# A two-layer hybrid trunk on one core: row vectors spread through DRAM, embedding blocks behind each gate, norm weights applied at PSUM

## The chip, the cores and the metric

The kernel runs on one core of one Trainium2 chip. The metric is the device time of one execution in microseconds (us). A core has a matrix engine (TensorE, PE in the profile; its weight loads are PEld), a vector engine (VectorE, DVE), an activation engine (ScalarE, ACT), a general engine (GpSimd, POOL) and queues that issue DMAs; here the queues of SyncE (SP) and of POOL are used. SBUF is the on-chip memory of 128 partitions, PSUM the memory that TensorE writes.

## The reference

256 tokens go through two layers of width 2048, batch 1. Each layer normalises, projects, mixes along the sequence, multiplies by a gate, projects back and adds; behind it comes a gated per-layer embedding.

```python
for i in range(DEPTH):                       # DEPTH = 2
    hn = rmsnorm(h, e_norm[j] if i % 2 == 0 else o_norm[j])
    if i % 2 == 0:                           # HGRN2 heads and RG-LRU blocks side by side
        qa, fa, ia, za, xb, zb = split(hn @ e_w_in[j])
        ya = head_rmsnorm(hgrn2(qa, fa, ia, lbs[j]), a_norm[j]) * silu(za)
        yb = rg_lru(causal_conv(xb, ...), ...) * silu(zb)
        mix = concat(ya, yb) @ e_w_out[j]
    else:                                    # mLSTM with a running-max stabiliser
        qk, v, og, z, ig, fg = split(hn @ o_w_in[j])
        q, k = split(silu(causal_conv(qk, ...)))
        yc = mlstm(q, k, v, ig + c_b_i[j], log_sigmoid(fg + c_b_f[j]))
        yc = head_rmsnorm(yc, c_norm[j]) * sigmoid(og) * silu(z)
        mix = yc @ o_w_out[j]
    h = h + mix
    pl = rmsnorm(p[i] @ ple_w[i], ple_norm[i])        # p[i]: 256 tokens x 256
    h = h + sigmoid(h @ ple_gate_w[i]) * pl
return rmsnorm(h, final_norm)
```

All of it is float32.

## The kernel before

Every weight comes from DRAM in raw halves of 128x1024 float32 through the SP queue (`raw`). ACT rounds a half to a shorter type (`whi`, L122) and DVE takes the rest (`wlo`, L123); activations are split likewise (`ahl`). A product is then three matmuls: hi×hi, hi×lo, lo×hi.

There are two shapes of product. `block` makes 128 features of all 256 tokens: 16 matmuls of 512 columns with `whi` (L153, both parts of the activation at once), a `pump()`, and 16 of 256 columns with `wlo` (L159). `project_tok` makes 512 features token by token, in two halves of 128 tokens; its matmuls of 512 columns are L194, L195 and L196.

Work beside the products is written as Python generators, called lanes: `start(name, gen)` enters one, `pump()` advances every lane by one `yield`, `drain(name)` runs one to its end. `pump()` is called once in each block and each group of `project_tok`, so a `yield` puts the next step about one block later. A tile scheduler and the order of the code set the order on each engine; an engine takes its instructions in that order, and waits at the head of its queue.

PSUM has three pools of 2 KB banks: `mm` (three banks, for the products), `mx` (three, for small products and transposes) and `st` (two).

What the change touches, in the order of time:

- Row norms. A norm factor is made with one token per partition (`rcr`). `to_free` lays it along the free axis on all partitions: DVE multiplies a diagonal (`dg`, L231), PE multiplies it by ones (L234), and `free_copy` copies the bank to SBUF on ACT (L262). It is used three times: `hrs` in layer 0 (first read by L176), `plrs` for the embedding of layer 0 (read by POOL, L341), `hrs` in layer 1 (first read at L835).
- Attention of layer 0. `attention(g)` makes the matrix `A` of two head groups; part of it, the cross-half product (L617 to L620), goes to a third `mx` bank. `read_out` multiplies the output `o` by its row norms `r` on POOL (L660). Beside it DVE runs the four-tap convolution (`xc`, L718), the products of the RG-LRU with its scan (`tt`, L706), and the weight subtractions; ACT waits for the scan in L688; PE's next product of `xc` is L684.
- The mixer of layer 1. Gate statistics give the running max `Mx` of eight heads (DVE, L844). `split8` rounds it into two parts (L242, L243), and for each head pair j `mix(j)` spreads two of its rows over all partitions with four matmuls by a column of an identity (`spread`, L250 and L251, into an `mx` bank); DVE then takes `wt` from it (L872).
- The `oz` gates of layer 1. For j = 0 to 3 `gate_tok` makes a gate `u` (DVE, L455), DVE multiplies it by the mixer's output (L981), and the lane `fm` (`feature_major`) transposes it on PE (L438, into `mx`) and evacuates it on ACT (L446) and DVE (L447) into `ahl`, which out_proj's blocks read. `embed(g)` makes 512 features of the embedding of layer 1, twelve matmuls in two halves (L964 to L966, into `mm`); DVE copies each half to `pl` (L968), ACT sums its squares (L970). Behind the gates POOL loads the embedding's norm row with `row` (L949, 512 KB each) and multiplies the eight halves by it (L993); the sums of squares are added on DVE (`total`, L999) and inverted.

The order around the gates, before:

```python
            start("fm", feature_major(u, "cn", 4 * j, y))
            if j in (1, 2):
                embed(j - 1)
        embed(2)
        pump()
        embed(3)
        drain("fm")
        pnr = row(0)
        ...
        act = out_proj(hq, a["oo"], y)
```

Of the kernel before, what the change touches and what calls it, by code (L numbers as in the profile page):

```python
# [19 lines left out]
P = 128  # L20
T = 256
# [23 lines left out]
def trunk(ctx: ExitStack, tc: tile.TileContext, a, out):  # L45
# [17 lines left out]
    def start(lane, gen):  # L63
        lanes.setdefault(lane, []).append(gen)
# [80 lines left out]

    def block(w, act):


        ps = pm.tile([P, 512], F32, name="mm", tag="mm")
        parts = load_weights(w)  # L150
        for k in range(KT):
            c = (k % 8) * P
            last["pe"] = te.matmul(ps, parts[k // 8][0][:, c:c + P],  # L153
                                   act[k // 2][2][:, (k % 2) * 512:(k % 2 + 1) * 512],
                                   start=(k == 0), stop=False).ins
        pump()
        for k in range(KT):
            c = (k % 8) * P
            last["pe"] = te.matmul(ps[:, T:2 * T], parts[k // 8][1][:, c:c + P], act[k // 2][0][:, k % 2],  # L159
                                   start=False, stop=(k == KT - 1)).ins  # L160
        return ps
# [65 lines left out]

    def to_free(rt):

        dg = tp.tile([P, T], F32, name="dg", tag="dg", bufs=1)  # L230
        v.tensor_tensor(out=dg.rearrange("p (h t) -> p h t", h=2), in0=ident.unsqueeze(1).to_broadcast([P, 2, P]),  # L231
                        in1=rt.unsqueeze(2).to_broadcast([P, 2, P]), op=ALU.mult)
        st = pst.tile([P, 512], F32, name="st", tag="st")
        te.matmul(st[:, 0:T], ones[:, 0:P], dg, start=True, stop=True)  # L234
        return st[:, 0:T]

    def split8(x, name):

        n = x.shape[0]
        hi = tp.tile([8, T], F32R, name=name + "h", tag="s8h", bufs=1)[0:n, :]  # L240
        lo = tp.tile([8, T], F32R, name=name + "l", tag="s8l", bufs=1)[0:n, :]
        v.tensor_copy(hi, x)  # L242
        v.tensor_tensor(out=lo, in0=x, in1=hi.bitcast(F32), op=ALU.subtract)  # L243
        return hi, lo

    def spread(o, parts, h):

        n = parts[0].shape[0]
        w = identr[0:n, h:h + 1].to_broadcast([n, P])
        te.matmul(o, w, parts[0], start=True, stop=False)  # L250
        te.matmul(o, w, parts[1], start=False, stop=True)  # L251

    def folded(acc, *more):
# [5 lines left out]
    def free_copy(rt, name):  # L259
        ps = to_free(rt)  # L260
        rs = tp.tile([P, T], F32, name=name, tag="rsb")
        s.copy(rs, ps)  # L262
        return rs
# [80 lines left out]

    def out_proj(hq, w, y):

        act = []
        for j in range(8):
            for i in range(2):
                ps = block(w[2 * j + i], y)  # L350
# [44 lines left out]
    pls = ple(load_p(0), p0, lambda: sy.dma_start(out=prm, in_=a["prm"]))  # L395
    identr = cp.tile([8, 8], F32R, name="identr")
    acc = cp.tile([P, 512], F32, name="acc", tag="acc")
# [62 lines left out]
    def derive():  # L460
        sy.dma_start(out=cst, in_=a["cst"])
        v.tensor_copy(identr, ident[0:8, 0:8])
        yield
# [33 lines left out]
    with m0_scope:  # L497
# [35 lines left out]
        A = m0.tile([P, 8, P], F32, name="A", tag="A", bufs=1)  # L533
        gp.memset(A, 0.0)

        def attention(g):
# [70 lines left out]
            for b in range(2):  # L607
# [8 lines left out]
                banks.append(p3)  # L616
            ps = px.tile([P, 512], F32, name="mx", tag="mx")  # L617
            for c in range(4):
# [19 lines left out]
        def read_out(g, A, Ac, vt):  # L638
# [20 lines left out]
            o8 = o.rearrange("p h (c e) -> p (h c) e", c=4)  # L659
            gp.tensor_tensor(out=o8, in0=o8, in1=r.unsqueeze(2).to_broadcast([P, 8, P]), op=ALU.mult)  # L660
            res["o", g] = o
# [107 lines left out]
    with tc.tile_pool(name="m1", bufs=2) as m1:  # L769
# [59 lines left out]
        def gate_stats(ps):  # L829
# [16 lines left out]
            s.activation(enm, enm, AF.Exp, scale=-1.0)  # L846
            pM.append(split8(Mx, "Mx"))
            yield
# [14 lines left out]
        den, ss, fac = (m1.tile([P, 16], F32, name=n, bufs=1) for n in ("den", "ss", "fac"))  # L863

        def mix(j):

            ps = px.tile([P, 512], F32, name="mx", tag="mx")
            for i in range(2):
                spread(ps[:, i * T:(i + 1) * T], pM[0], 2 * j + i)
            p3 = ps.rearrange("p (i t) -> p i t", i=2)  # L870
            wt = m1.tile([P, 2, 384], F32, name="wt", tag="wt", bufs=1)
# [3 lines left out]
            for i in range(2):  # L875
                hd = 2 * j + i
                s.activation(wt[:, i, 0:T], wt[:, i, 0:T], AF.Exp, bias=aT[:, hd:hd + 1])
                s.activation(wt[:, i, T:384], wt[:, i, T:384], AF.Exp, bias=aT[:, 8 + hd:9 + hd])
            yield
            yield  # L880
# [74 lines left out]

        def embed(g):
            hi, lo = load_weights(a["pw1"][g // 2], halves=(g % 2,))[0]
            halves = []
            for hf in range(2):
                ps = pm.tile([P, 512], F32, name="mm", tag="mm")  # L960
                for k in range(2):
# [5 lines left out]
                pl = m1.tile([P, 512], F32, name="pl", tag="qk", bufs=8)  # L967
                v.tensor_copy(pl, ps)  # L968
                sq = tp.tile([P, 512], F32, name="sq", tag="sq")
# [4 lines left out]
        for j in range(4):  # L974
# [8 lines left out]
            start("fm", feature_major(u, "cn", 4 * j, y))  # L983
            if j in (1, 2):
                embed(j - 1)
        embed(2)
        pump()
        embed(3)
        drain("fm")
        pnr = row(0)  # L990
        for g in range(4):
            for pl in pls[g]:
                gp.tensor_tensor(out=pl, in0=pl, in1=pnr[g // 2][:, (g % 2) * 512:(g % 2 + 1) * 512], op=ALU.mult)  # L993
        fnr = row(1)

# [7 lines left out]
        rp = m1.tile([P, 2], F32, name="rp", bufs=1)  # L1003
        v.tensor_scalar(rp, rsqrt_cols(total(pss, 4)), 0.5, None, op0=ALU.mult)

        act = out_proj(hq, a["oo"], y)


# [195 lines left out]
```

## Time and profile before

| what | value |
|---|---|
| median of 3 runs (lowest to highest) | 1090.41 us (1090.06 to 1091.36) |
| the profiled execution | 1090.81 us, its span 1089.0 us |
| mean granted TensorE clock | 0.997 |
| PE busy | 1064.6 us, 98% of the span |
| DVE, ACT, POOL busy | 753.4, 580.8, 86.5 us (69%, 53%, 8%) |
| mean traffic | 184 GB/s; the 16 DMA engines are 40% to 80% busy by slice |

A line of the timeline has the start in us from the span's start, the time of the group in us, engine, line, operation, the tile written and the tiles read, shapes, and how many instructions the group has; in brackets stands how long the engine was idle before it, and what ended that. Consecutive matmuls overlap in their records, so what one costs is the distance from its start to the next one's. A line of groups has the count, then busy time and the mean duration in ns, then the idle time before. Where three durations stand with slashes, they are the shortest, the median and the longest.

### The profile page before, as it was taken

To read this page: it belongs to the slowest core of one execution; us is meant where nothing else is said; L and a number is where in the kernel's file an instruction comes from. 1 tells how busy PE (TensorE), PEld (TensorE's weight loads), DVE (VectorE), ACT (ScalarE), POOL (GpSimd) and SP (SyncE) were. 2 spreads that over 40 slices of the span, in tenths; PEclk is the share of its full clock that TensorE was granted. 3 is DMA by queue.
4 is the path that set the end of the run, shared out by engine and by line. 5 is a ranking of instruction groups with operands and counts; after the bars stand their busy time and mean duration, and the time that the engine had idled before them with its cause. 6 is when DMAs were issued, how large, how long until landed. Compare 5 with 4: busy or idle time off the path is not lost.

```text
span 1089.0 us, 16844 instructions
## 1 busy us (share of the span) xinstructions
PE 1064.6 (98%) x6522; PEld 913.0 (84%) x6522; DVE 753.4 (69%) x1121; ACT 580.8 (53%) x850; POOL 86.5 (8%) x74
## 2 busy tenths in 40 slices
PE   7999999999999999999999999999999999999996
PEld 6788888887888888888888888888888878888886
DVE  7968978877767556877544877764456686655565
ACT  6565455688654435555444656644445554434543
POOL 2142200000000000112000000000000120000111
PEclk9999999999999999999999999999999999999998
DMA  8655544446755555555554544445555665555552
GB/s 322 204 193 193 176 161 140 148 136 194 236 198 186 192 192 192 187 186 184 190 193 166 180 156 157 163 168 194 196 190 199 217 202 177 183 189 175 192 174 78
DMA packets 55952, 200.31 MB, mean 184 GB/s; under 512 B 6208, under 2 KB 6592, under 8 KB 55872
## 3 DMA queue, kind: packets, MB, share of 16 engines
q1 hardware_dynamic: 54720, 195.04, 53.0%
q0 software_dynamic: 1152, 4.19, 1.2%
q8 instruction: 51, 0.84, 0.3%
q14 instruction: 29, 0.24, 0.1%
HBM read 197.11 MB, written 2.10 MB: 183 GB/s over the span
## 4 chain that ended last, share of the span: by engine, by line
PE 89%; DVE 5%; ACT 4%; issue 1%; DMA 1%; SPq 0%; DVEq 0%; ACTq 0%
PE mm L153 31%; PE mm L159 17%; PE mm L194 12%; PE mm L196 12%; PE mm L195 12%; DVE wlo L123 2%; ACT whi L122 1%; PE mm L1058 1%; PE mm L1056 1%; PE mm L1057 1%; DMA raw<-in_pw_dram 1%; PE nu L897 1%; PE mx L556 1%; DVE ahl L138 0%; ACT L695 0%
## 5 line engine op out<-in xcount | busy, mean ns | idle before, releaser
L123 DVE TENSOR_TENSOR wlo<-raw,whi 128x1024 fp32r<-128x1024 f32 (+1 forms) x361 | 450.7, 1273 | 244.8 <-ACT whi L122 136.1
L122 ACT CAST whi<-raw 128x1024 fp32r<-128x1024 f32 (+1 forms) x361 | 377.1, 1047 | 331.8 <-PE mm L153 171.8
L153 PE MATMUL mm<-ahl,whi 128*128 128x512 f32 x1536 | 367.7, 392 | 2.7 <-DVE ahl L447 1.9
L153 PEld LDWEIGHTS mm<-ahl,whi 128*128 128x128 f32 x1536 | 282.3, 188 | 59.1 <-DVE ahl L447 3.0
L194 PE MATMUL mm<-whi,ahl 128*128 128x512 f32 x608 | 239.8, 394 | 2.4 <-DVE u L455 1.9
L196 PE MATMUL mm<-whi,ahl 128*128 128x512 f32 x608 | 237.1, 390 | 1.8 <-DVE ahl L138 1.8
L195 PE MATMUL mm<-wlo,ahl 128*128 128x512 f32 x608 | 237.2, 390 | 0.8 <-DVE wlo L123 0.8
L159 PE MATMUL mm<-ahl,wlo 128*128 128x256 f32 x1536 | 202.4, 285 | 0.0
L159 PEld LDWEIGHTS mm<-ahl,wlo 128*128 128x128 f32 x1536 | 195.4, 191 | 6.2
L194 PEld LDWEIGHTS mm<-whi,ahl 128*128 128x128 f32 x608 | 114.3, 188 | 27.6 <-DVE u L455 3.1
L196 PEld LDWEIGHTS mm<-whi,ahl 128*128 128x128 f32 x608 | 114.2, 188 | 27.0 <-DVE ahl L138 3.1
L195 PEld LDWEIGHTS mm<-wlo,ahl 128*128 128x128 f32 x608 | 114.3, 188 | 23.9 <-DVE wlo L123 1.1
L165 ACT COPY sm<-mm 128x256 f32<-128x256 f32 x64 | 23.7, 371 | 45.0 <-PE mm L159 45.0
L271 POOL TENSOR_TENSOR acc<-acc,sq 128x512 f32<-128x512 f32 x11 | 19.9, 1812 | 212.6 <-ACT sq L270 212.4
L166 DVE TENSOR_TENSOR mg<-mm,sm 128x256 f32<-128x256 f32 x64 | 26.7, 418 | 0.0
L782 DVE SCALAR_TENSOR_TENSOR qk<-mg,prm,qk 128x255 f32<-128x255 f32 (+2 forms) x48 | 21.3, 479 | 6.8 <-ACT qk L779 6.5
L949 POOL DMA_DIRECT2D row<-in_rows_dram x4 | 2.2, 553 | 279.8 <-DVE u L981 268.1
L1044 POOL TENSOR_TENSOR pl<-pl,row 128x512 f32<-128x512 f32 x6 | 9.2, 1533 | 153.7 <-ACT sq L1028 153.7
L446 ACT ACTIVATE ahl<-mx,prm 128x256 fp32r<-128x256 f32 x24 | 10.9, 473 | 14.6 <-PE mx L438 8.3
L1056 PE MATMUL mm<-whi,ahl 128*128 128x256 f32 x64 | 18.3, 286 | 0.0
L138 DVE TENSOR_TENSOR ahl<-hq,ahl 128x512 fp32r<-128x512 f32 x16 | 10.7, 690 | 10.8 <-ACT ahl L137 10.8
L1057 PE MATMUL mm<-wlo,ahl 128*128 128x256 f32 x64 | 18.1, 283 | 0.0
(299 smaller groups left out, 822.8 us busy)
## 6 DMA issues: line engine op xcount, KB each, us to landing
raw<-in_ew_dram SPq DMA_DIRECT2D x64, 512.0 KB, 4.8
raw<-in_g_dram SPq DMA_DIRECT2D x56, 512.0 KB, 4.3
raw<-in_eo_dram SPq DMA_DIRECT2D x32, 512.0 KB, 4.6
raw<-in_ov_dram SPq DMA_DIRECT2D x32, 512.0 KB, 4.1
raw<-in_oqk_dram SPq DMA_DIRECT2D x32, 512.0 KB, 4.5
raw<-in_oog_dram SPq DMA_DIRECT2D x32, 512.0 KB, 4.2
raw<-in_oz_dram SPq DMA_DIRECT2D x32, 512.0 KB, 4.1
raw<-in_oo_dram SPq DMA_DIRECT2D x32, 512.0 KB, 4.6
```

Of the source, the lines that this page charges most:

```text
L122: last["act"] = s.copy(h, r).ins
L123: last["dve"] = v.tensor_tensor(out=l, in0=r, in1=h.bitcast(F32), op=ALU.subtract).ins
L153: last["pe"] = te.matmul(ps, parts[k // 8][0][:, c:c + P], act[k // 2][2][:, (k % 2) * 512:(k % 2 + 1) * 512], start=(k == 0), stop=False).ins
L159: last["pe"] = te.matmul(ps[:, T:2 * T], parts[k // 8][1][:, c:c + P], act[k // 2][0][:, k % 2], start=False, stop=(k == KT - 1)).ins
L165: s.copy(small, ps[:, T:2 * T])
L166: v.tensor_tensor(out=dst, in0=ps[:, 0:T], in1=small, op=ALU.add)
L194: te.matmul(ps[hf], xh, wh, start=(k == 0), stop=False)
L195: te.matmul(ps[hf], xh, wl, start=False, stop=False)
L196: last["pe"] = te.matmul(ps[hf], xl, wh, start=False, stop=(k == KT - 1)).ins
L782: v.scalar_tensor_tensor(dst[:, sh:T], pi[:, 0:T - sh], pc("ccw", k * 16 + b), dst[:, sh:T], op0=ALU.mult, op1=ALU.add)
L1056: te.matmul(ps[hf], xh, wh, start=(k == 0), stop=False)
L1057: te.matmul(ps[hf], xh, wl, start=False, stop=False)
```

## The change

`to_free`, `split8`, `spread` by matmul and the identity for it are gone. `free_copy` and the mixer's spread write the row vector to a DRAM tile and read it back with every partition reading the same bytes, both on POOL's DMA queue. `mix(0)` has one more `yield` ahead of its work, and the spread of pair j + 2 is asked for when pair j's `wt` is done. `embed(j)` stands behind each gate j and writes `st` banks; its norm row is loaded per block (256 KB, `pnr`) and multiplied where the bank is evacuated, so POOL's eight products are gone. The row of the final norm, the sums and the inversion go into a lane that runs during out_proj. The last gate's `fm` lane is finished within out_proj's first block, which runs twelve hi matmuls, then the lane, then the rest. The cross-half product of attention writes an `st` bank, and the product of `o` with its row norms is made by DVE. Line numbers after the change differ by up to 15: L153 is L155, L159 is L162, L123 is L124, L438 is L427, L447 is L436, L455 is L444, L718 is L707, L706 is L695, L964 to L966 are L969 and the next.

```diff
-    def block(w, act):
+    def block(w, act, mid=None):
...
+        if mid is None:
+            his(range(KT))
+            pump()
+            los(range(KT))
+        else:
+            his(range(12))
+            mid()
+            los(range(12))
+            his(range(12, KT))
+            los(range(12, KT))
         return ps
...
     def free_copy(rt, name):
-        ps = to_free(rt)
+        d = dr.tile([T], F32, name=name + "d", tag="rsd")
+        gp.dma_start(out=d.rearrange("(h p) -> p h", h=2), in_=rt)
         rs = tp.tile([P, T], F32, name=name, tag="rsb")
-        s.copy(rs, ps)
+        gp.dma_start(out=rs, in_=d.partition_broadcast(P))
         return rs
...
-            ps = px.tile([P, 512], F32, name="mx", tag="mx")
+            ps = pst.tile([P, 512], F32, name="st", tag="st")
             for c in range(4):
                 cc = slice(c * P, (c + 1) * P)
                 te.matmul(ps[:, cc], kx[:, cc], qx[:, cc], start=True, stop=True)
...
-            gp.tensor_tensor(out=o8, in0=o8, in1=r.unsqueeze(2).to_broadcast([P, 8, P]), op=ALU.mult)
+            v.tensor_tensor(out=o8, in0=o8, in1=r.unsqueeze(2).to_broadcast([P, 8, P]), op=ALU.mult)
...
-            pM.append(split8(Mx, "Mx"))
+            d = dr.tile([8, T], F32, name="Mxd", tag="Mxd")
+            gp.dma_start(out=d, in_=Mx)
+            pM.append(d)
...
+        def spread(j):
+            t = m1.tile([P, 2, T], F32, name="spr", tag="spr", bufs=2)
+            gp.dma_start(out=t, in_=pM[0][2 * j:2 * j + 2].partition_broadcast(P))
+            spr[j] = t
+
         def mix(j):
 
-            ps = px.tile([P, 512], F32, name="mx", tag="mx")
-            for i in range(2):
-                spread(ps[:, i * T:(i + 1) * T], pM[0], 2 * j + i)
-            p3 = ps.rearrange("p (i t) -> p i t", i=2)
+            if j == 0:
+                spread(0)
+                spread(1)
+                yield
+            p3 = spr[j]
...
+            if j < 2:
+                spread(j + 2)
...
         def embed(g):
+            pnr = m1.tile([P, 512], F32, name="pnr", tag="spr", bufs=2)
+            gp.dma_start(out=pnr, in_=a["rows"][0, g * 512:(g + 1) * 512].partition_broadcast(P))
...
-                ps = pm.tile([P, 512], F32, name="mm", tag="mm")
+                ps = pst.tile([P, 512], F32, name="st", tag="st")
...
-                v.tensor_copy(pl, ps)
+                v.tensor_tensor(out=pl, in0=ps, in1=pnr, op=ALU.mult)
...
-            if j in (1, 2):
-                embed(j - 1)
-        embed(2)
+            embed(j)
         pump()
-        embed(3)
-        drain("fm")
-        pnr = row(0)
-        for g in range(4):
-            for pl in pls[g]:
-                gp.tensor_tensor(out=pl, in0=pl, in1=pnr[g // 2][:, (g % 2) * 512:(g % 2 + 1) * 512], op=ALU.mult)
-        fnr = row(1)
+        pump()
+        pump()
+        rows = []
...
-        v.tensor_scalar(rp, rsqrt_cols(total(pss, 4)), 0.5, None, op0=ALU.mult)
-
-        act = out_proj(hq, a["oo"], y)
+        def embed_norm():
+            yield
+            yield
+            rows.extend(row(1))
+            v.tensor_scalar(rp, rsqrt_cols(total(pss, 4)), 0.5, None, op0=ALU.mult)
+            yield
+
+        start("en", embed_norm())
+        act = out_proj(hq, a["oo"], y, lambda: drain("fm"))
+        drain("en")
+        fnr = rows
```

On PE, at the end of the gates of layer 1, the order before the change is this: the last embedding block, the transposes of `u` between and behind its matmuls, and out_proj's first two blocks.

```order
L438 MATMUL mx<-cst,u 128x128
L964 MATMUL mm<-whi,ahl 128x512
L965 MATMUL mm<-wlo,ahl 128x512
L966 MATMUL mm<-whi,ahl 128x512
L964 MATMUL mm<-whi,ahl 128x512
L965 MATMUL mm<-wlo,ahl 128x512
L966 MATMUL mm<-whi,ahl 128x512
L438 MATMUL mx<-cst,u 128x128 x5
L153 MATMUL mm<-ahl,whi 128x512 x21
L159 MATMUL mm<-ahl,wlo 128x256 x16
L153 MATMUL mm<-ahl,whi 128x512 x11
L159 MATMUL mm<-ahl,wlo 128x256 x16
```

At the same place on PE after the change:

```order
L427 MATMUL mx<-cst,u 128x128 x2
L155 MATMUL mm<-ahl,whi 128x512 x6
L427 MATMUL mx<-cst,u 128x128 x3
L155 MATMUL mm<-ahl,whi 128x512 x5
L427 MATMUL mx<-cst,u 128x128 x3
L155 MATMUL mm<-ahl,whi 128x512
L162 MATMUL mm<-ahl,wlo 128x256 x12
L155 MATMUL mm<-ahl,whi 128x512 x9
L162 MATMUL mm<-ahl,wlo 128x256 x4
L155 MATMUL mm<-ahl,whi 128x512 x11
L162 MATMUL mm<-ahl,wlo 128x256 x16
```

The transposes now stand among out_proj's first twelve hi matmuls, in pieces of two, three and three, and the four remaining hi matmuls, which read the last transposed columns, behind twelve lo matmuls.

On DVE, in layer 0, around the second head group's `read_out` (`hnr` holds its row norms), before the change:

```order
L123 TENSOR_TENSOR wlo<-raw,whi 128x1024 x2
L658 TENSOR_SCALAR hnr<-hnr,rth 128x4 x2
L718 SCALAR_TENSOR_TENSOR xc<-mg,prm,xc 128x255 x2
L718 SCALAR_TENSOR_TENSOR xc<-mg,prm,xc 128x254 x2
L718 SCALAR_TENSOR_TENSOR xc<-mg,prm,xc 128x253 x2
L706 SCALAR_TENSOR_TENSOR tt<-av,it 128x1024
L123 TENSOR_TENSOR wlo<-raw,whi 128x1024 x4
```

At the same place on DVE after the change:

```order
L124 TENSOR_TENSOR wlo<-raw,whi 128x1024 x2
L647 TENSOR_SCALAR hnr<-hnr,rth 128x4 x2
L707 SCALAR_TENSOR_TENSOR xc<-mg,prm,xc 128x255
L649 TENSOR_TENSOR o<-o,hnr 128x1024
L707 SCALAR_TENSOR_TENSOR xc<-mg,prm,xc 128x254
L707 SCALAR_TENSOR_TENSOR xc<-mg,prm,xc 128x255
L707 SCALAR_TENSOR_TENSOR xc<-mg,prm,xc 128x253
L707 SCALAR_TENSOR_TENSOR xc<-mg,prm,xc 128x254
L695 SCALAR_TENSOR_TENSOR tt<-av,it 128x1024
L124 TENSOR_TENSOR wlo<-raw,whi 128x1024 x2
L707 SCALAR_TENSOR_TENSOR xc<-mg,prm,xc 128x253
L124 TENSOR_TENSOR wlo<-raw,whi 128x1024 x2
```

The product of `o` now stands among the convolution's steps, and the last of these has moved behind the scan and a pair of weight subtractions.

More of the change, by code (lines that the diff above doesn't have):

```diff
@@ L56, in trunk @@
     pst = ctx.enter_context(tc.tile_pool(name="pst", bufs=2, space=PSUM))
+    dr = ctx.enter_context(tc.tile_pool(name="dr", bufs=2, space=bass.MemoryType.DRAM))
     lanes = {}
@@ L144, in mm3, with his, los @@
         last["pe"] = te.matmul(o, wlo, x[0][:, k], start=False, stop=end).ins
-    def block(w, act):
+    def block(w, act, mid=None):
         ps = pm.tile([P, 512], F32, name="mm", tag="mm")
         parts = load_weights(w)
[L151 to L160, printed above, removed]
+        def his(ks):
+            for k in ks:
+                c = (k % 8) * P
+                last["pe"] = te.matmul(ps, parts[k // 8][0][:, c:c + P],
+                                       act[k // 2][2][:, (k % 2) * 512:(k % 2 + 1) * 512],
+                                       start=(k == 0), stop=False).ins
+        def los(ks):
+            for k in ks:
+                c = (k % 8) * P
+                last["pe"] = te.matmul(ps[:, T:2 * T], parts[k // 8][1][:, c:c + P], act[k // 2][0][:, k % 2],
+                                       start=False, stop=(k == KT - 1)).ins
+        if mid is None:
[8 more added lines that the diff above has]
+            los(range(12, KT))
         return ps
@@ L226, in rs_tok @@
         return rsqrt_cols(y)
[L228 to L251, printed above, removed]
     def folded(acc, *more):
@@ L343, in ple_norm, with out_proj @@
                 yield
-    def out_proj(hq, w, y):
+    def out_proj(hq, w, y, mid=None):
         act = []
@@ L349, in out_proj @@
             for i in range(2):
-                ps = block(w[2 * j + i], y)
+                ps = block(w[2 * j + i], y, mid if i == j == 0 else None)
                 hh = pair_of(hq, j)[:, i * T:(i + 1) * T]
@@ L395, in trunk @@
     pls = ple(load_p(0), p0, lambda: sy.dma_start(out=prm, in_=a["prm"]))
-    identr = cp.tile([8, 8], F32R, name="identr")
     acc = cp.tile([P, 512], F32, name="acc", tag="acc")
@@ L461, in derive @@
         sy.dma_start(out=cst, in_=a["cst"])
-        v.tensor_copy(identr, ident[0:8, 0:8])
         yield
@@ L533, in trunk @@
         A = m0.tile([P, 8, P], F32, name="A", tag="A", bufs=1)
-        gp.memset(A, 0.0)
         def attention(g):
@@ L542, in attention @@
             v.tensor_tensor(out=qf, in0=q, in1=f, op=ALU.mult)
+            if g == 0:
+                gp.memset(A, 0.0)
             yield
@@ L863, in trunk @@
         den, ss, fac = (m1.tile([P, 16], F32, name=n, bufs=1) for n in ("den", "ss", "fac"))
-        def mix(j):
-            ps = px.tile([P, 512], F32, name="mx", tag="mx")
-            for i in range(2):
-                spread(ps[:, i * T:(i + 1) * T], pM[0], 2 * j + i)
-            p3 = ps.rearrange("p (i t) -> p i t", i=2)
+        spr = {}
+        def spread(j):
+            t = m1.tile([P, 2, T], F32, name="spr", tag="spr", bufs=2)
+            gp.dma_start(out=t, in_=pM[0][2 * j:2 * j + 2].partition_broadcast(P))
+            spr[j] = t
+        def mix(j):
+            if j == 0:
[3 more added lines that the diff above has]
+            p3 = spr[j]
             wt = m1.tile([P, 2, 384], F32, name="wt", tag="wt", bufs=1)
```

## The prediction

> **What bounds the kernel now.** I read the page's busy times first, then the waits of TensorE, then the timeline around every place that the diff touches.
>
> ```profile
> PE 1064.6 (98%) x6522; PEld 913.0 (84%) x6522; DVE 753.4 (69%) x1121; ACT 580.8 (53%) x850; POOL 86.5 (8%) x74
> ...
> PE mm L194 <- DVE u L455: 1.9, 3, 1.2
> PE mm L153 <- DVE ahl L447: 1.9, 2, 1.7
> ...
> 100.00:117.00 17.00, 17.00 (x100) 15.04 (x99) 14.93 (x10) 8.05 (x11) 14.81 (x8) 1.00 0.41 133
> 592.00:700.00 108.00, 108.00 (x622) 94.79 (x621) 84.46 (x144) 68.85 (x127) 0.00 (x0) 1.00 0.51 168
> ```
>
> TensorE is busy for 98% of the span, at a granted clock of 1.00 in the stretches shown, so the time is the number of its instructions times their step, plus the waits listed (us in total, times, longest). The last window row (span, then PE, PEld, DVE, ACT, POOL, clock, DMA share) says that around the first spreads PE has no gap at all, while DVE has 23.5 us of slack and ACT 39: there an instruction taken from PE is time taken from the kernel. So I price the change by what it removes from PE's own queue, by start-to-start distances, since the busy columns of neighbouring matmuls overlap.
>
> **The change part by part.** The unit is the step from one matmul to the next.
>
> ```profile
> 47.59 0.39 PE L195 MATMUL mm<-wlo,ahl 128*128 128x512 f32 x1
> 47.82 0.39 PE L196 MATMUL mm<-whi,ahl 128*128 128x512 f32 x1
> 48.15 0.70 PE L234 MATMUL st<-dg,ones 128*128 128x256 f32 x2
> ...
> 48.92 0.40 PE L195 MATMUL mm<-wlo,ahl 128*128 128x512 f32 x1
> ...
> 78.88 3.82 PE L153 MATMUL mm<-ahl,whi 128*128 128x512 f32 x16
> ...
> 84.45 1.78 PE L153 MATMUL mm<-ahl,whi 128*128 128x512 f32 x7
> ...
> 96.03 3.82 PE L153 MATMUL mm<-ahl,whi 128*128 128x512 f32 x16
> ...
> 102.04 2.22 PE L153 MATMUL mm<-ahl,whi 128*128 128x512 f32 x9
> ...
> 618.42 3.82 PE L153 MATMUL mm<-ahl,whi 128*128 128x512 f32 x16
> ...
> 624.83 1.55 PE L153 MATMUL mm<-ahl,whi 128*128 128x512 f32 x6
> L250 PE MATMUL mx<-Mxh,identr x8: 271/325/377, 622.2 to 702.7; 8*128 8x256 f32 x8
> L234 PE MATMUL st<-dg,ones x6: 376/381/484, 48.1 to 528.4; 128*128 128x256 f32 x6
> ```
>
> Steps of 512 columns are 0.23 us (47.59 to 47.82). An undisturbed block, 16 hi and 16 lo matmuls, lasts 84.45 − 78.88 = 5.57 us.
>
> *Spread of the running max.* A block with the four spread matmuls in it lasts 624.83 − 618.42 = 6.41 us, 0.84 more. The row of L250 counts eight, two to each head pair, so there are four such blocks: 4 × 0.84 = **3.4 us** that go. Two tiny casts (L242 and L243) leave DVE, which has slack there.
>
> *Row norms to the free axis (`to_free`).* In token-major code, 47.82 to 48.92 is 1.10 us for two ordinary steps (0.45) and the two matmuls: 0.65. In the block at 96.03 it is 6.01 − 5.57 = 0.44. The third, at 528, I put between them, at the lower end: 0.44. Sum **1.5 us**; with it go a DVE product and an ACT copy each, off the path.
>
> What comes instead is DMA on POOL's queue, in two hops, so each use gets a wait with a cover:
>
> ```profile
> DMA to landing us min/median/max: 4.3/6.0/7.6
> L176 DVE TENSOR_TENSOR mg<-mg,hrs x25: 420/692/1330, 84.4 to 703.0; 128x512 f32<-128x512 f32 x23, 128x256 f32<-128x256 f32 x2
> 607.69 0.67 DVE L844 TENSOR_TENSOR_SCAN Mx<-ones,li 8x256 f32<-8x256 f32 x1
> 622.92 0.69 DVE L872 TENSOR_TENSOR wt<-cst,mx 128x512 f32<-128x512 f32 x1
> 101.33 14.81 POOL L341 TENSOR_TENSOR pl<-pl,plrs 128x512 f32<-128x512 f32 x8 [22.48 <-ACT plrs L262]
> L123 DVE TENSOR_TENSOR wlo<-raw,whi 128x1024 fp32r<-128x1024 f32 x5 | 11.1, 2256 | 3.1 <-ACT plrs L262 3.1
> L123 DVE TENSOR_TENSOR wlo<-raw,whi x361: 692/1225/2362, 5.0 to 1069.6; 128x1024 fp32r<-128x1024 f32 x180, 128x512 fp32r<-128x512 f32 x1
> ```
>
> The first line is of the only POOL-queue loads of this size class near the new ones (the row loads, L949): 4.3 to 7.6 us from issue to landing. The first `hrs` is ready to leave at about 48 and is read by DVE at 84.4: 36 us for two hops of at most 15.2. The second has from 528 to 598. The running max is done at 608.36 and its first reader, `wt`, stands at 622.92: 14.6 us, against 8.6 to 15.2 for two hops, so the wait lies between 0 and 0.6; the mixer starts a pump, thus a block (5.57), later now, which closes even that. Behind `wt` on DVE stand weight subtractions for PE, so a miss would be paid. `plrs` is behind the eight POOL products of L341, whose results are wanted only by the embedding's gate hundreds of microseconds on; two hops move them by at most some 10 us. But while they run, five weight subtractions of DVE take 2256 ns each instead of the 1225 of the median (last two rows, the first of them for 100 to 117 alone); PE was busy for 17.00 of 17.00 there, so the same burden at another time costs nothing either, unless it meets attention (R2). I put the DMAs at 0.
>
> *Embedding blocks.*
>
> ```profile
> 826.56 0.39 PE L196 MATMUL mm<-whi,ahl 128*128 128x512 f32 x1
> 826.79 1.03 PE L438 MATMUL mx<-cst,u 128*128 128x128 f32 x8
> ...
> 827.90 0.40 PE L195 MATMUL mm<-wlo,ahl 128*128 128x512 f32 x1
> ...
> 838.33 0.39 PE L966 MATMUL mm<-whi,ahl 128*128 128x512 f32 x1
> 839.05 0.50 PE L194 MATMUL mm<-whi,ahl 128*128 128x512 f32 x1 [0.33 <-DVE u L455]
> 839.38 0.40 PE L195 MATMUL mm<-wlo,ahl 128*128 128x512 f32 x1
> ...
> 865.05 0.50 PE L194 MATMUL mm<-whi,ahl 128*128 128x512 f32 x1 [0.33 <-DVE u L455]
> ...
> 887.85 0.39 PE L964 MATMUL mm<-whi,ahl 128*128 128x512 f32 x1
> ...
> 900.71 1.65 PE L153 MATMUL mm<-ahl,whi 128*128 128x512 f32 x6 [1.69 <-DVE ahl L447]
> ...
> 909.71 0.63 PE L153 MATMUL mm<-ahl,whi 128*128 128x512 f32 x2
> 897.60 2.47 DVE L999 TENSOR_TENSOR pss<-pss 128x2 f32<-128x2 f32 x2
> ...
> 895.32 4.73 POOL L993 TENSOR_TENSOR pl<-pl,row 128x512 f32<-128x512 f32 x3 [1.64 <-DVE pl L968]
> ```
>
> From the first embedding matmul after gate 3 (887.85) to the end of out_proj's second block (909.71) are 21.86 us. The work in it without waits: 24 embedding matmuls 5.44, two blocks 11.14, eight transposes 0.89 (826.56 to 827.90, less two steps): 17.47. So **4.39 us** are lost there. The rows say how: POOL's products of L993 run at 895.32 to 900.05, and in that time two sums of two columns (L999) take 2.47 us; behind them on DVE stands the evacuation L447, for which PE waits 1.69. After the change POOL has no product there, the sums come later in out_proj, twelve embedding matmuls instead of 24 stand in the stretch, and the first block runs twelve hi matmuls before it needs the last transposed columns. What stays: PE's transposes stand in pieces of 2, 3 and 3, which costs 0.3 to 0.8 over one group, and the gate's last `u` is still made by DVE behind a pair of weight subtractions. Counting from the end of gate 3 with durations of DVE's rows, I find the last two transpose groups ready about 0.4 to 1.5 us ahead of PE. Bounds 0 and 4.39; I take **3.8**.
>
> The embedding takes a third `mm` bank now; at 839.05 PE waits because gate `u` has not been read out of the others: 838.33 to 839.38 is 1.05 for two steps, 0.60 lost, and again, a gate later, at 865.05 in the same form (three such waits in the list, 1.9 us in total, the third is elsewhere). With the embedding in `st` banks both go: **1.2** (0 at the least, if an `st` bank comes free late; its last user is a whole gate, 865.05 − 839.05 = 26 us, earlier). The norm row is a 256 KB load on POOL's queue, issued a gate ahead; 7.6 against 26. The product at PSUM replaces a copy of the same size: 0.
>
> *Attention's product from POOL to DVE.*
>
> ```profile
> 212.81 2.96 DVE L718 SCALAR_TENSOR_TENSOR xc<-mg,prm,xc 128x255 f32<-128x255 f32 x6 [1.51 <-ACT xc L715]
> ...
> 237.07 4.09 DVE L718 SCALAR_TENSOR_TENSOR xc<-mg,prm,xc 128x255 f32<-128x255 f32 x6
> ...
> 237.31 2.00 POOL L660 TENSOR_TENSOR o<-o,hnr 128x1024 f32<-128x1024 f32 x1 [57.46 <-ACT av L688]
> ...
> 243.40 0.47 ACT L688 ACTIVATE it<-mx,prm 128x256 f32<-128x256 f32 x1 [3.33 <-DVE tt L706]
> ```
>
> Six conv steps take 2.96 us alone and 4.09 beside POOL's product. On DVE the product costs about one 128x1024 pass, 1.22 (the median of L123), so DVE's queue grows by 0.1; one conv step now stands behind the scan and a weight pair, so the scan that ACT waited 3.33 for starts some 0.4 earlier, but the last `xc` may come up to 1.9 late for PE. The end of this stretch (205 to 262) waits on ACT's backlog. Bounds −1.9 and +1.1; I take **0.3**. [...]
>
> Sum: 3.4 + 1.5 + 3.8 + 1.2 + 0.3 = 10.2. Against the profiled execution (1090.81 us, span 1089.0, which is 0.40 above the median of the runs, 1090.41) this gives **1080.6 us**.
>
> **Rivals.**
> R1, the wait at the end of the embedding only changes its name: PE reaches the last transposes while DVE is still behind with `u` and evacuations, for gate `u`, the norm product and two weight pairs (2 × 1.22 each) share DVE there. For it: my margin is 0.4 us. Against: the POOL products that doubled DVE's durations are gone. The 3.8 is lost, 1084.4.
> R2, attention gets worse: the late `xc` (1.9), and POOL's L341 moved onto the start of attention, where weight subtractions at 2.26 instead of 1.22 delay `qf` by about one such (1.0). Instead of +0.3 this is −2.9: 1083.8.
> R3, slower: `wt` heads DVE's queue and waits for the two hops of the running max. It decides once both together take over 14.6 + 10.2 = 24.8 us, 12.4 a hop; with 13.5 each the wait is 12.4 and the end 1093.0. Against: the slowest POOL-queue landing in the trace is 7.6; for: no row shows an element-wise write to DRAM. [...]
> R4, the removal buys nothing, because DVE and ACT bound the stretches in truth and PE's gaps come back as waits for weights: 1090.8. Against: PE 108.00 of 108.00, with DVE 84.46.
>
> **How the numbers follow.** Forecast 0.63, R1 0.20, R2 0.10, R3 0.03, R4 0.04. Low end: every term at its best, 3.5 + 1.5 + 4.4 + 1.2 + 1.1 = 11.7, 1079.1, and a little below for waits that vanish elsewhere: 1078.5. High end: R1 and R2 together, 10.2 − 3.8 − 3.2 = 3.2, 1087.6; I stop at 1086.5, since both at once is unlikely. This leaves some 0.12 outside. 0.2% is 2.2 us, what a measurement can tell here; faster by more 0.93 (forecast, R1, R2), same 0.04, slower 0.03.
>
> **What would show it.** PE's matmul count down by 22; blocks near 620 at 5.57; no step over 0.3 at 48, 99, 528; no wait of L194 behind the embedding blocks; from gate 3's end to the end of out_proj's second block about 4 us less; DVE's `wt` without a long wait ahead. I am wrong if PE waits for the fm lane in out_proj's first block, for `xc` near 245, or DVE for `spr`.

## The result, and the profile after

The changed kernel takes 1083.93 us (median of 4 runs, 1081.78 to 1085.16), the kernel before 1090.53 beside it (4 runs); the ratio is 0.9934, with a 95% interval of 0.9922 to 0.9945. So it is 6.6 us faster, where 1080.6 us and a gain of 10.2 were forecast. The time lies in the range and the sign is as forecast, but a third of the gain is missing. The profiled execution took 1084.92 us, its span 1083.2. Its runs scatter by 3.4 us; the mean granted clock of TensorE was 0.995 in three of them and 0.998 in the fastest, which is taken up at the end.

First the page's busy times, then the waits of TensorE in the changed kernel (us in total, times, longest).

```profile
PE 1060.7 (98%) x6500; PEld 913.9 (84%) x6500; DVE 743.4 (69%) x1117; ACT 580.4 (54%) x847; POOL 76.7 (7%) x77
```

```profile
PE mm L143 <- ACT whi L123: 6.9, 2, 5.8
PE mx L673 <- DVE xc L707: 2.3, 1, 2.3
PE mx L545 <- DVE qf L529: 1.9, 1, 1.9
PE mm L208 <- ACT ahl L138: 1.2, 1, 1.2
PE mm L210 <- DVE ahl L139: 1.1, 1, 1.1
```

The 22 matmuls are gone (6522 to 6500), and so are the waits for `u` and those at the end of the gates. In their place stand two waits that the list of before did not have: for `qf`, at the start of attention, and for `xc`, in the stretch of the RG-LRU.

Where the time came from is read by setting the start of the same matmul in both traces side by side, the k-th hi matmul of a block or the k-th of `project_tok`, and noting by how much the difference changes from one place to the next. All places are on the axis of before.

| place | what is there | after − before | forecast |
|---|---|---|---|
| up to 47 | start, first loads | +1.32 | 0 |
| 48 to 49; 96 to 102; 528 to 529 | the three row norms (B) | −0.67, −0.47, −0.42 = −1.56 | −1.5 |
| 102 to 126 | start of attention | +3.59 | 0, and 1.0 in R2 |
| 126 to 208 | rest of attention | −0.30 | 0 |
| 208 to 264 | convolution, RG-LRU, gates (E) | −0.20 | −0.3 |
| 529 to 730 | spread of the running max (A) | −3.40 | −3.4 |
| 839 and 865 | the two waits for `u` (D) | −0.48, −0.63 = −1.11 | −1.2 |
| 865 to 905 | end of the gates (C), less one embedding block that had moved ahead | −4.35 | −3.8 |
| 905 to the end | | +0.09 | 0 |
| sum | | −5.92 | −10.2 |

Four terms of the sum came out within 0.1, the fifth half a microsecond better. The row of C holds 0.13 that belongs to the last wait for `u`: counted from the matmul behind each wait instead of the one that waited, D is 1.24 and C 4.22. The blocks at the place of the first spread last 626.84 − 621.27 = 5.57 us, and `wt` has no wait ahead of it:

```profile
621.27 3.82 PE L155 MATMUL mm<-ahl,whi 128*128 128x512 f32 x16
...
626.84 3.82 PE L155 MATMUL mm<-ahl,whi 128*128 128x512 f32 x16
...
610.54 0.67 DVE L833 TENSOR_TENSOR_SCAN Mx<-ones,li 8x256 f32<-8x256 f32 x1
...
623.78 0.68 DVE L871 TENSOR_TENSOR wt<-cst,spr 128x512 f32<-128x512 f32 x1
```

The four reads of the running max, by their line (durations of the issue in ns, first and last start), and their landing:

```profile
L860 POOL DMA_DIRECT2D spr<-Mxd x4: 537/538/551, 616.0 to 648.6; - x4
...
DMA to landing us min/median/max: 3.8/4.4/5.6
```

The last embedding block and out_proj's first two blocks now stand like this on PE:

```profile
888.78 0.39 PE L967 MATMUL st<-whi,ahl 128*128 128x512 f32 x1
...
891.51 0.38 PE L427 MATMUL mx<-cst,u 128*128 128x128 f32 x2
891.65 1.64 PE L155 MATMUL mm<-ahl,whi 128*128 128x512 f32 x6
893.12 0.49 PE L427 MATMUL mx<-cst,u 128*128 128x128 f32 x3
893.37 1.40 PE L155 MATMUL mm<-ahl,whi 128*128 128x512 f32 x5
894.61 0.49 PE L427 MATMUL mx<-cst,u 128*128 128x128 f32 x3
...
903.73 3.59 PE L155 MATMUL mm<-ahl,whi 128*128 128x512 f32 x15
```

From 888.78 to 903.73 are 14.95 us for twelve embedding matmuls (2.72), two blocks (11.14) and eight transposes (0.89), together 14.75: 0.2 us lost where 4.39 were lost before, and no bracket with a wait in it.

The larger missing part stands at the start of attention. On POOL, DVE and PE of the changed kernel:

```profile
97.76 0.74 POOL L250 DMA_DIRECT2D plrsd<-rcr  x1 [15.53 <-DVE rcr L222]
106.27 0.55 POOL L252 DMA_DIRECT2D plrs<-plrsd  x1 [7.77 <-DMA plrsd<-rcr]
112.14 14.26 POOL L331 TENSOR_TENSOR pl<-pl,plrs 128x512 f32<-128x512 f32 x8 [5.32 <-DMA plrs<-plrsd]
...
112.65 4.11 DVE L124 TENSOR_TENSOR wlo<-raw,whi 128x1024 fp32r<-128x1024 f32 x2 [2.93 <-issue]
...
123.08 2.18 DVE L529 TENSOR_TENSOR qf<-q,f 128x1024 f32<-128x1024 f32 x1
...
122.66 0.77 PE L540 MATMUL mx<-q,k 128*32 128x32 f32 x64
125.31 0.74 PE L545 MATMUL mx<-qf,k 128*32 128x16 f32 x64 [1.88 <-DVE qf L529]
```

The windows right behind the two new waits (span, busy times of PE, PEld, DVE, ACT and POOL with their instructions, then the granted clock, DMA share and GB/s):

```profile
125.90:129.40 3.50, 3.50 (x33) 3.47 (x22) 3.50 (x5) 0.00 (x0) 0.50 (x1) 0.51 0.16 55
248.80:252.30 3.50, 3.50 (x9) 2.76 (x10) 0.00 (x0) 2.37 (x4) 0.00 (x0) 0.51 0.67 233
```

The two hops of `plrs` take from 97.76 to 112.14, so POOL's eight products start 10.8 us later than the 101.33 of before and reach to 126.4. `qf`, 1.22 us before, takes 2.18 among them, after `tot` (1.44, 0.68 before), `mg` (1.78, 0.68 before) and `q` (2.18, 0.88 before), and PE waits 1.88. Right behind each of the waits the granted clock is 0.51 for 3.4 us, which costs PE by estimate about half of them: the sixteen matmuls of L162 behind the first wait take 3.65 us, where such a group takes 2.08. The first hop of a row norm, the write of 256 single elements, lands late (three uses, line L250):

```profile
DMA to landing us min/median/max: 8.2/9.4/10.1
```

### The profile page after: what moved, and what is told of

Its sections match the earlier page's. It is cut to its first block, busy times and chain, and to the rows that moved or that the text cites. A ratio compares the mean times of both kernels' runs of the same rounds, so it can differ in the third digit from the quotient of the medians.

```text
span 1083.2 us, 16792 instructions
## 1 busy us (share of the span) xinstructions
PE 1060.7 (98%) x6500; PEld 913.9 (84%) x6500; DVE 743.4 (69%) x1117; ACT 580.4 (54%) x847; POOL 76.7 (7%) x77
## 4 chain that ended last, share of the span: by engine, by line
PE 92%; DVE 3%; ACT 2%; issue 1%; DMA 0%; SPq 0%; DVEq 0%; ACTq 0%
PE mm L155 31%; PE mm L162 16%; PE mm L208 12%; PE mm L210 12%; PE mm L209 12%; DVE wlo L124 1%; PE mm L1064 1%; PE mm L1063 1%; PE mm L1062 1%; PE nu L898 1%; PE mx L545 1%; ACT whi L123 1%; DMA raw<-in_pw_dram 0%; PE mx L427 0%; DVE hn L267 0%
## 5 line engine op out<-in xcount | busy, mean ns | idle before, releaser
L124 DVE TENSOR_TENSOR wlo<-raw,whi 128x1024 fp32r<-128x1024 f32 (+1 forms) x361 | 445.7, 1258 | 255.8 <-ACT whi L123 147.3
L123 ACT CAST whi<-raw 128x1024 fp32r<-128x1024 f32 (+1 forms) x361 | 377.4, 1048 | 332.7 <-PE mm L155 163.4
L155 PE MATMUL mm<-ahl,whi 128*128 128x512 f32 x1536 | 367.8, 391 | 0.0
L155 PEld LDWEIGHTS mm<-ahl,whi 128*128 128x128 f32 x1536 | 282.0, 188 | 55.8 <-DVE ahl L139 0.6
L208 PE MATMUL mm<-whi,ahl 128*128 128x512 f32 x608 | 239.5, 394 | 1.2 <-ACT ahl L138 1.2
L209 PE MATMUL mm<-wlo,ahl 128*128 128x512 f32 x608 | 237.1, 390 | 0.0
L162 PE MATMUL mm<-ahl,wlo 128*128 128x256 f32 x1536 | 203.3, 285 | 0.0
L162 PEld LDWEIGHTS mm<-ahl,wlo 128*128 128x128 f32 x1536 | 197.2, 192 | 6.2
L208 PEld LDWEIGHTS mm<-whi,ahl 128*128 128x128 f32 x608 | 114.5, 188 | 25.2 <-ACT ahl L138 1.6
L209 PEld LDWEIGHTS mm<-wlo,ahl 128*128 128x128 f32 x608 | 114.5, 188 | 23.1
L1062 PE MATMUL mm<-whi,ahl 128*128 128x256 f32 x64 | 18.3, 285 | 0.0
L1064 PE MATMUL mm<-whi,ahl 128*128 128x256 f32 x64 | 18.1, 283 | 0.0
L190 DVE TENSOR_TENSOR mg<-mg,hrs 128x512 f32<-128x512 f32 (+1 forms) x25 | 17.8, 713 | 0.3
L143 PE MATMUL mm<-ahl,whi 128*128 128x256 f32 x32 | 10.6, 332 | 6.9 <-ACT whi L123 6.9
```

The source lines that it names most:

```text
L123: last["act"] = s.copy(h, r).ins
L124: last["dve"] = v.tensor_tensor(out=l, in0=r, in1=h.bitcast(F32), op=ALU.subtract).ins
L155: last["pe"] = te.matmul(ps, parts[k // 8][0][:, c:c + P], act[k // 2][2][:, (k % 2) * 512:(k % 2 + 1) * 512], start=(k == 0), stop=False).ins
L208: te.matmul(ps[hf], xh, wh, start=(k == 0), stop=False)
L209: te.matmul(ps[hf], xh, wl, start=False, stop=False)
L1062: te.matmul(ps[hf], xh, wh, start=(k == 0), stop=False)
```

## The experiments

Two theories were set against each other. H: POOL's products by `plrs`, late by two DMA hops, meet attention's start and slow DVE there. J: the shortfall is a late start and scatter. For attention's second half there was a third question, whether the wait for `xc` is a loss of its own.

**1. `plrs` back on PE.** In the changed kernel `free_copy` branches for this one use:

```diff
     def free_copy(rt, name):
+        if name == "plrs":
+            rs = tp.tile([P, T], F32, name=name, tag="rsb")
+            s.copy(rs, to_free(rt))
+            return rs
         d = dr.tile([T], F32, name=name + "d", tag="rsd")
```

> The changed kernel, with the embedding norm factor of layer 0 (plrs) spread by the diagonal, the two matmuls and the ACT copy of the kernel before; the other two row norms stay on the DRAM path. Theory H (the two DRAM hops of plrs move POOL's eight products from 101 to 112, onto the start of attention, where they slow DVE, PE waits 1.9 us for qf and its granted clock is halved for 3.4 us after): the products are back at about 101, no wait for qf, no halved clock near 126; 3.6 us back, 0.44 paid for the matmuls, so about 1081 against 1084. Rival J (the shortfall is a late start and scatter between runs, and attention is as it was): 1084.4. Rival R2b (DVE is late at qf anyway, for other work that the change put there): the qf wait stays, 1084.4.

Measured: 1080.14 us (1078.35 to 1081.96), ratio to before 0.9902 (0.9889 to 0.9915). The products start at 101.03 again, and the list of PE's waits is this:

```profile
101.03 15.90 POOL L344 TENSOR_TENSOR pl<-pl,plrs 128x512 f32<-128x512 f32 x8 [19.51 <-ACT plrs L260]
```

```profile
PE mm L143 <- ACT whi L123: 6.2, 2, 5.7
PE mx L686 <- DVE xc L720: 2.3, 1, 2.3
PE mm L208 <- ACT ahl L138: 1.2, 1, 1.2
PE mm L210 <- DVE ahl L139: 1.1, 1, 1.1
```

The wait for `qf` is not in the list, and 3.8 us are back by the medians. H holds, J can at most be the small rest. The wait for `xc` is as long as it was.

**2. Row norms through DRAM alone.** The kernel before, with only the new `free_copy`.

> The kernel before, with only the three row norms sent through DRAM on POOL's queue. Theory H: saves 1.5 us of matmuls on PE and loses about 3.6 at the start of attention, so about 2 us slower than before, 1092.6. Rival J: the removal counts alone, 1089.0. Rival that the loss needs the whole change: 1089.0 as well, with no wait for qf.

Measured: 1092.04 us (1091.15 to 1094.66), ratio 1.0012 (1.0004 to 1.0021): slower by 1.3 against the 1090.76 beside it. The part of the change that looked like a pure saving of 1.5 us is a loss by itself, with the same wait:

```profile
111.63 14.25 POOL L343 TENSOR_TENSOR pl<-pl,plrs 128x512 f32<-128x512 f32 x8 [5.10 <-DMA plrs<-plrsd]
...
124.80 0.74 PE L558 MATMUL mx<-qf,k 128*32 128x16 f32 x64 [1.88 <-DVE qf L544]
```

Here the clock stayed at 1.00 behind the wait (124 to 131 in the profiled execution), which fits a loss smaller than expected. The two slowest of its eleven runs (1094.66 and 1093.55) are those with the lowest mean clock, 0.995 and 0.996.

**3. The product of `o` back on POOL.** In the changed kernel the multiplication by the row norms is given to `gp` again instead of `v`.

> The changed kernel, with the product of the attention output and its row norms back on POOL. My reckoning (term E about 0: the wait of PE for xc, 2.3 us, stands in place of waits of the same sum later in the same stretch, which ACT sets): the xc wait goes, waits of L208 and L209 near 259 to 264 come back, the time stays within 1 us of 1084. Rival (the late xc step and the halved clock behind it are a pure loss): 1.5 to 4 us faster, 1080 to 1082.5.

Measured: 1084.66 us (1083.01 to 1087.1), ratio 0.9949 (0.9936 to 0.9961), the same as the change within a microsecond. The wait for `xc` is gone and waits of L208 for ACT (1.2 us) and of L209 for DVE's `wlo` (0.8) are back in the same stretch; the wait for `qf` is there too, with 1.2 us. By itself this reads as if ACT's backlog set the end whatever DVE does; run 8 says otherwise.

**4. The products later in the code.** Thirty-four `yield`s in place of one between `free_copy` and the products.

> The changed kernel, DRAM path kept for all three row norms, with POOL's eight products by plrs put 34 pumps later, behind attention. Theory H in the form that contention between POOL's products and DVE's passes costs, not the hops themselves: no qf wait, 3.6 us back, and nothing paid, about 1080.4; DVE's weight passes in 100 to 126 at 1.2 us. Rival (the hops hold up something else, such as POOL's or DVE's queue): the qf wait stays, 1084. Rival (the products do as much harm where they now run): about 1083.

Measured: 1084.66 us (1082.52 to 1085.27), ratio 0.9941 (0.9929 to 0.9953). This says nothing on contention, for the products still run as soon as `plrs` lands, and the wait for `qf` is there (1.3 us):

```profile
115.09 14.91 POOL L332 TENSOR_TENSOR pl<-pl,plrs 128x512 f32<-128x512 f32 x8 [5.72 <-DMA plrs<-plrsd]
```

POOL's queue had nothing ahead of the products that would hold them: it had been idle for 5.72 us when `plrs` landed. They began 2.95 us later than in the changed kernel (112.14), with a first hop that was issued 1.99 later (99.75 against 97.76); the later place in the code was no later time here.

**5. The products tied to a later result.** The DRAM path stays for all three row norms; a DVE pass makes the factor of the products depend on the second scan.

```diff
-        rs = free_copy(rt, "plrs")
+        rc = free_copy(rt, "plrs")
+        while ("h", 1) not in res:
+            yield
+        rs = tp.tile([P, T], F32, name="plrt", tag="plrt", bufs=1)
+        v.scalar_tensor_tensor(rs, res["h", 1][:, 0:T], 0.0, rc, op0=ALU.mult, op1=ALU.add)
         yield
```

> The changed kernel with the DRAM path kept for all three row norms, and POOL's eight products by plrs made to depend on the second RG-LRU scan (DVE adds zero times its result to plrs, one more pass of 256 columns), so that they run behind attention, at some 270 us. The run before this one had only moved them in the code, and they ran at 115 all the same, since nothing stood ahead of them in POOL's queue. Theory H, contention: no wait for qf, DVE's weight passes at 1.2 us in 100 to 126, about 1080 (3.6 us less than the change). Rival, the two hops alone hold attention up: qf wait stays, 1084. Rival, the harm moves with the products: qf wait gone, new waits of PE behind 270, 1082 to 1084.

Measured: 1079.9 us (1079.29 to 1081.4), ratio 0.9901 (0.9884 to 0.9918).

On POOL, DVE and PE:

```profile
104.35 0.56 POOL L252 DMA_DIRECT2D plrs<-plrsd  x1 [7.90 <-DMA plrsd<-rcr]
...
118.28 1.23 DVE L533 TENSOR_TENSOR qf<-q,f 128x1024 f32<-128x1024 f32 x1
...
123.34 0.19 PE L549 MATMUL mx<-qf,k 128*32 128x16 f32 x1
...
270.91 14.90 POOL L335 TENSOR_TENSOR pl<-pl,plrt 128x512 f32<-128x512 f32 x8 [115.27 <-DVE plrt L331]
```

The hops are as slow as before (the second is issued 7.9 us after POOL began to wait), `qf` is ready at 119.5, 3.8 us ahead of PE, which takes it at 123.34, and 4.0 us are back. So it is the meeting of POOL's products and DVE's passes that costs, not the DMA. Behind 270 the same products, 14.90 us of POOL, cost PE no wait: its list has the two for the first weights (6.4 us), one for `xc` (2.3) and two for split activations (1.2 and 1.1), all ahead of them.

**6. The spread alone.** The kernel before, with the running max through DRAM.

> The kernel before, with only the spread of the running max sent through DRAM. By term A of the prediction 3.4 us less, 1087.3, and DVE's wt without a wait for the tile; the two hops of 8.6 us are under the cover. Rival: wt heads DVE's queue late and part of it is given back, 1088 to 1090.

Measured: 1087.52 us (1086.26 to 1088.46), ratio 0.9972 (0.9961 to 0.9982). By the trace the difference grows by 3.40 between 529 and 730, the term to the digit; by the medians it is 3.0.

**7. The embedding alone.** The kernel before, with the blocks behind each gate in `st` banks, the norm row at PSUM, the lane and the split first block.

> The kernel before, with only the embedding part: a block behind each gate in st banks, the norm row applied at PSUM, the lane in out_proj, out_proj's split first block. By terms C and D 5.0 us less, and by the trace of the whole change 5.4 (5.45 between 729 and 905): about 1085.2. Rival, that part of the 5.4 came with the other edits: 1087 or more.

Measured: 1085.83 us (1085.49 to 1086.44), ratio 0.9958 (0.9943 to 0.9973): 4.7 less than before beside it, and 5.49 by the trace between 729 and 905; in the profiled execution a start that is 1.1 later takes part of it back. The gain of this part doesn't need the other edits.

**8. `plrs` on PE, and the product of `o` one pump later.** A `yield` ahead of the multiplication, which stays on DVE.

```diff
-            read_out(g, A, Ac, vts[g])
+            o, r = read_out(g, A, Ac, vts[g])
+            yield
+            o8 = o.rearrange("p h (c e) -> p (h c) e", c=4)
+            v.tensor_tensor(out=o8, in0=o8, in1=r.unsqueeze(2).to_broadcast([P, 8, P]), op=ALU.mult)
+            res["o", g] = o
```

> The changed kernel with plrs spread by PE as in the first run, and with the product of the attention output and its row norms (on DVE) one pump later, behind the convolution and ahead of the scan. If the late xc is a loss of its own, the wait of 2.3 us for xc goes and nothing comes back: about 1078. If ACT's backlog in that stretch sets its end, the wait turns up again at 255 to 260 as waits of L208 and L209, and the time is that of the first run, 1080 to 1081.

Measured: 1078.27 us (1078.04 to 1079.38), ratio 0.989 (0.9875 to 0.9905). ACT's pass that had waited for the scan, first in the changed kernel, then in this run, and the window 205 to 262 of this run:

```profile
245.98 0.84 ACT L677 ACTIVATE it<-mx,prm 128x256 f32<-128x256 f32 x2 [2.13 <-DVE tt L695]
```

```profile
245.01 0.84 ACT L692 ACTIVATE it<-mx,prm 128x256 f32<-128x256 f32 x2
```

```profile
205.00:262.00 57.00, 57.00 (x406) 48.88 (x395) 43.95 (x71) 54.32 (x100) 0.57 (x1) 1.00 0.45 149
```

Both sets of waits are gone, those for `xc` and those behind 255. Against run 1 the trace gains 2.6 us at the place of the wait for `xc` (241 to 246) and loses 0.1 behind it. PE is busy for 57.00 of 57.00, where it was busy for 53.99 before. All six convolution steps stand together ahead of the product, and ACT has other work in front of the passes that had waited for the scan; it idled 3.33 us at that place before, 2.13 in the changed kernel, and not at all here. That the backlog behind 255 was the echo of this idle time fits these rows, but ACT's own order changed as well in this run, and no run moved its passes alone.

**9. Run 8 with the small identity cast back.** DVE gets the 8x8 cast again that `derive` did at the start; nothing reads its result.

> The kernel of the last run of the second set (plrs by PE, product of o one pump later), with the small cast for the 8x8 identity, which nothing reads any more, put back on DVE at the start. In every kernel without that cast PE waits 1.3 to 1.4 us near 28 for a split activation, and in those with it 0.3 to 0.4: there DVE's four hn passes take 3.25 us instead of 1.12, beside a POOL product of the same time. Theory (the missing cast moves DVE onto POOL's product): wait back at 0.4, 0.9 us faster, 1077.4. Rival (the start is scatter in the loads): within 0.3 us of 1078.3.

**10. Run 5 with run 8's later product.** The two edits together, without any matmul for row norms.

> The changed kernel with plrs by DRAM and its products behind the second scan (as in the first run of the second set), and the product of o one pump later. The two gains add: no wait for qf, none for xc, no matmul for plrs: 0.4 us less than 1078.3, about 1077.9. Rival: the products behind the scan now meet the product of o or the gate passes on DVE, 1079 to 1080.

**11. Run 10 with the identity cast back.**

> The kernel before this one with the small identity cast back on DVE at the start. If both ideas hold, the fastest of all: about 1077.0. If the cast does nothing: 1077.9.

Measured, beside 1091.13 of before: run 9 takes 1077.49 us (ratio 0.9875, 0.986 to 0.989), run 10 1077.03 (0.9875, 0.9859 to 0.9892), run 11 1076.92 (0.9868, 0.9854 to 0.9883). Run 10 fits the sum of the two gains, with 0.9 more than was expected, within its scatter. All three beat both kernels, run 11 by 13 to 16 us against before by its interval.

On the cast the trace and the times do not agree. DVE and POOL near 28 us in run 9:

```profile
28.18 1.12 DVE L280 TENSOR_SCALAR hn<-xq,prm 128x256 f32<-128x256 f32 x4
26.80 5.35 POOL L274 TENSOR_TENSOR acc<-acc,sq 128x512 f32<-128x512 f32 x2 [2.82 <-ACT sq L273]
```

The same in run 10:

```profile
27.13 3.24 DVE L267 TENSOR_SCALAR hn<-xq,prm 128x256 f32<-128x256 f32 x4
25.75 3.94 POOL L261 TENSOR_TENSOR acc<-acc,sq 128x512 f32<-128x512 f32 x2 [2.69 <-ACT sq L260]
```

And a line of PE's waits in run 11:

```profile
PE mm L210 <- DVE ahl L139: 1.8, 2, 1.1
```

With the cast DVE's four passes take 1.12 us and POOL is the slower one, without it 3.24. The wait of PE there is 0.3 in run 9 and 1.2 in run 10. But run 11, with the cast, has a wait of the same kind some microseconds earlier instead (last row: two waits, 1.8 us in total), and gains 0.1 over run 10, while run 9 gains 0.8 over run 8 with intervals that overlap. Something else may hang on the cast: in the profiled executions of runs 5 and 8, which lack it, PE's waits near 29 were followed by a halved clock (last section). Whether the cast is worth anything stays open; the +1.32 of the start in the table is partly this and partly the first matmul, which began between 4.9 and 6.3 us in these profiles with no order that follows the edits.

## Why the prediction was right or wrong

**Right, with their sizes.** A (3.4, measured 3.40, and alone in run 6), B's matmuls (1.5, measured 1.56), D (1.2, measured 1.11). C was put at 3.8 between 0 and 4.39 and measured 4.35, or 4.22 without the part that belongs to D: the cost that I let stand for transposes in pieces, 0.3 to 0.8 by my estimate, for which I had given no row, was 0.2: the stretch took 14.95 us, with the eight in pieces, against 14.75 with the 0.89 of one group. R1 did not happen; PE waited nowhere in out_proj's first block. R3 did not happen: the running max lands in 4.2 and is read back in at most 5.6, so `wt` had about 2 us to spare (616.0 + 5.6 against 623.78; the second hop's issue is at 616.0).

**Wrong: the step on `plrs`.** The prediction took the two hops at 15.2 us at most, said that they move the products by at most some 10 us, and that "the same burden at another time costs nothing either, unless it meets attention (R2)". The two hops of `plrs` kept to that sum (14.4 us, from 97.76 to 112.14), and the products moved by 10.8, about as far as was said; they met attention. So what failed is the price of nothing that this shift was given. The bound of one hop failed too: the first was put at 7.6, from row loads, and measured 8.2 to 10.1. R2 named this place and this mechanism, but with a chance of 0.10 and 1.0 us as its price. Measured are 1.88 us of wait and some 1.6 us of halved clock behind it, most of the 3.59 in the table, and 3.8 and 4.0 are back in runs 1 and 5. The margin to look at was in the trace of before:

```profile
121.50 1.22 DVE L542 TENSOR_TENSOR qf<-q,f 128x1024 f32<-128x1024 f32 x1
...
123.03 0.19 PE L556 MATMUL mx<-qf,k 128*32 128x16 f32 x1
```

`qf` was ready 0.3 us ahead of PE, and POOL's products ended at 116.1 (101.33 + 14.81), 5.4 us before `qf` began. A shift of ten microseconds had to cross that.

That the time fell into the range all the same is partly luck. The high end had been made from R1, which didn't happen, and R2; the loss at attention and the later start took up that room. R2's 1083.8 is almost the measured 1083.93, but of its 2.9 us the late `xc` had 1.9, where the table has 0.20 gained for that stretch, and the start of attention 1.0, where it has 3.59. Halved clocks, and the start, had no place in the sum.

The size of the slowing is in the traces: `qf` took 2.18 us beside POOL's products and 1.23 without them (run 5). How the two engines hold each other up was not shown.

The first hop of a row norm moves 1 KB and landed after 8.2 to 10.1 us; the first hop of the running max, 8 KB from the same queue, landed after 4.2. The slow one writes 256 single elements; that it is their count, and not something else in that queue, was not tried by itself.

**Right in sum, wrong in reason: E.** The term was 0.3, measured 0.20. The late `xc` cost 2.31, a little over its bound of 1.9, and the waits behind 255 went in exchange. I gave ACT's backlog as what sets the end of this stretch, and run 3 fitted that. Run 8 shows that the backlog is no fixed limit: with the product placed behind the convolution, PE has no wait in this stretch at all. That it came from ACT's idle time at the scan is the reading that fits, not a thing tried by itself. The bound of +1.1 for this term was too low; run 8 is 1.9 faster than run 1 by the medians.

**The start** (+1.32) was not in the sum. It is of the size of the scatter of the first loads (the first matmul began between 4.9 and 6.3 us) and was not explained.

The sum with these corrections: 10.2 − 3.59 − 1.32 + 0.55 (C) and + 0.08 for the rest is 5.92, as the table has it; the median of the runs is 0.7 better than the profiled pair.

## What to carry to other kernels

Sending the row vectors through DRAM took matmuls of 1.56 and 3.40 us off the matrix engine here, but `plrs` came 14.4 us after its first hop was issued; look at who runs beside its reader then, not only at whether the reader can wait. POOL's products, on an idle engine, started when their input landed, at 115.09, though they stood 34 yields behind it in the code (run 4); to keep such work off a place, tie it to a result that comes later (at 270.91 in run 5). Where waits add up at the end of a stretch, look for the first idle time of the engine that is behind: putting the product of `o` behind the convolution removed the wait of 2.3 us for `xc` and left none behind 255 (run 8), while giving it to POOL put waits of 1.2 and 0.8 us in its place (run 3).

## What the runs showed that was not expected

Some waits of PE were followed by a halved clock: after the waits of 1.88 and 2.31 us in the changed kernel the granted clock was 0.51 for 3.4 us each. Two shorter waits close together were followed by the same: 1.24 and 0.76 us in run 3, whose rows come first here, and 1.25 and 1.09 us in run 8 (columns as above). Run 5 has such a pair near 29 too (1.2 and 1.1 us).

```profile
255.22:258.63 3.41, 1.53 (x6) 0.69 (x4) 1.84 (x2) 3.41 (x6) 0.00 (x0) 1.00 0.69 232
258.63:262.05 3.42, 3.30 (x8) 2.30 (x8) 3.30 (x6) 3.40 (x7) 0.00 (x0) 0.50 0.62 184
```

```profile
27.70:31.10 3.40, 1.55 (x6) 0.98 (x7) 3.40 (x7) 2.76 (x5) 1.25 (x1) 1.00 0.46 149
31.10:34.50 3.40, 3.40 (x10) 2.66 (x9) 3.40 (x9) 2.28 (x5) 0.00 (x0) 0.50 0.47 141
```

It does not always happen: the same waits had no such window in the profiled executions of run 1 (`xc`, at a clock of 1.00 from 205 to 262, and the pair near 29) and run 2 (`qf`, 1.00 from 124 to 131), nor had the pair near 29 in the changed kernel (1.16 and 1.09 us, at 1.00 from 28 to 40), and the waits of the kernel before behind its first loads, up to 1.69 us, had none (1.00 from 12 to 1082.2). In the traces the halved stretches of one execution stand on a fixed beat: those of the changed kernel last from 125.94 to 129.36 and from 248.82 to 252.24, 3.41 us each, and begin 122.88 us apart, which is 36 times 3.413; a third one, behind PE's last matmul, begins at 1078.26, 243 times 3.413 later; and those of run 5, at 30.80 and 245.84, are 63 times apart. So it may matter how much idle time falls into one beat, which no run tried by itself. The wait for `qf` in run 2 lay across an edge of the beat, at 124.05; but the wait for `xc` in run 1 had 1.9 of its 2.3 us in one beat and no halved clock behind it, so this alone does not explain it, and what does was not shown.

The halved clock fits the scatter of the changed kernel's runs, the fastest of which (1081.78) is the only one with a mean clock of 0.998, though one with 0.995 took 1082.94; the windows of those runs are not known one by one. So idle time of this length costs itself and, in some executions, by estimate about 1.7 us more (half of 3.4).
